# First k group of a hybrid decoder layer in seven products, their sums in three PSUM banks

## The chip, the cores and the metric

One core of one Trainium2 chip runs the whole layer. The metric is device time in microseconds, the median of several runs. The engines are named as the profile names them: PE is TensorE, DVE VectorE, ACT ScalarE, POOL GpSimd, SP SyncE.

## What is computed

The sizes: 512 tokens, model width 2048, 16 heads of 64, all in float32. The reference, cut:

```python
h = rms_norm(x, norm_g)
z = h @ w_in                       # 2048 -> 7 x 1024
a_val, a_glu, a_gate, q, k, v, b_gate = jnp.split(z, SPLIT_POINTS, axis=-1)
u = a_val * jax.nn.sigmoid(a_glu)
u = causal_depthwise_conv(u, conv_w, conv_b)              # 31 taps
u = jax.nn.silu(layer_norm(u, conv_norm_g, conv_norm_b))
u = u @ conv_pw_w + conv_pw_b
y_a = u * jax.nn.silu(a_gate)
q = rms_norm(q.reshape(bsz, s, N_HEADS, HEAD_DIM), q_norm_g)
k = rms_norm(k.reshape(bsz, s, N_HEADS, HEAD_DIM), k_norm_g)
o = dilated_attention_mixture(q, k, v)                    # windows (128,1) (512,4) (2048,16)
y_b = o.reshape(bsz, s, ATTN_WIDTH) * jax.nn.silu(b_gate)
y = x + jnp.concatenate([y_a, y_b], axis=-1) @ w_out
```

## The kernel before

**Matrix products.** Each float32 operand is split into a high and a low float16 part, and a product is three matmuls: high × high, high × low, low × high (`tri`, L409). The columns of the weights are worked off in groups of 512, in the order of GROUPS (L48): vg0 to vg3 (GLU value and gate), q0, k0, v0, bg0 (gate of attention), q1, k1, v1, ag0, ag1 (gate of the convolution branch), bg1, pw0, pw1 (pointwise), then the groups of the output product. vg0 and vg1 are done otherwise, in exact float32 parts.

An ordinary group has 4 units of 8 slots, one unit for 512 rows of weights (a tile wf, 1 MB). A slot is 6 matmuls of 512 columns (`slot_matmuls`, L884), so a group has 192. The weights of the next unit are split during a unit: ScalarE writes the high part wh (`split_hi`, L299), VectorE the low part wl (`split_lo`, L307), 2048 elements a partition each.

A group of SEVEN (L53: vg3, q0, v0) multiplies in halves of blocks: the weights give four blocks a11, a12, a21, a22, the activations b11 to b22, and seven products of sums of them stand for eight of blocks (`input_products`, L1106 to 1270). Each product has two pairs of 512 rows and two halves m, so 28 steps of 12 matmuls of 256 columns, 336. s1 to s4 are sums of weight blocks, t1 to t4 of activation blocks (`sum_x`, computed once, kept in tx). The sums s2, s3, s4 are made by accumulating DMAs that POOL issues (L1122), s1 by VectorE. For each product and pair ScalarE writes the high part (L1128) and VectorE, a step later, the low part of the weights, both named ws and 1024 wide; high parts are issued 5 steps ahead of the matmuls that read them. They come from a pool of four buffers. The products lie in banks of PSUM (lin_ps, four banks, tile ps_l), and are joined to the four output blocks cb by VectorE (`stt`, one operand in PSUM) and by copies of ScalarE (L1180).

**Norms of q and k.** `norm_qk` (L470 to 497): VectorE sums squares by head (`reduce`, tile ss), POOL scales and takes the power −1/2 (L478, L168), VectorE scales (cb or z times ss), ScalarE and VectorE write high and low parts qhl, SP transposes them. The four steps are due at the four delays of n, in slots.

**What sets the order.** One program is written out in one order; each engine takes its own instructions in that order. `clock[0]` counts slots; `after(n, fn)` puts work into a calendar for n slots later. A seven-product group counts 28 steps on 32 slots. Attention over half of the heads (`attention`, L792) is entered in the calendar when its k group has been issued, and starts at least 28 slots later.

The depthwise convolution is a generator (`conv`, from L537): 240 steps cv<-u,cw,cv on VectorE, then sums, LayerNorm (mean, squares lnsq, second moments, lnrow), the silu (L601) and the split into u16 (L314 high, then low). `run_conv` (L847) draws steps in each slot. A counter V.load adds an estimate of nanoseconds for every VectorE instruction, and each call takes PACE (1230; PACE_2, 1480, once attention has begun) off it; steps are drawn while it is below zero. So the convolution fills what the groups leave of VectorE. A seven-product group calls it 28 times and an ordinary one 32 times. Ahead of each unit of pw0, `while need not in u16: next(convolution)` issues whatever is still missing of the first four u16, in one go.

In bg0, bg1, ag0 and ag1 ScalarE takes the silu of each output tile (gate, L465); in bg1 VectorE then multiplies it by the attention output and ScalarE sums its squares (junk<-gate, L190), which it does for the weights too (junk<-wf, called wsum in the order).

Of the kernel before, what the change touches and what calls it, by code (L numbers as in the profile page):

```python
# [12 lines left out]
F16 = mybir.dt.float16  # L13
# [6 lines left out]
P = 128  # L20
S = 512
D = 2048
C = 1024
# [29 lines left out]
SEVEN = (("vg", 3), ("q", 0), ("v", 0))  # L53
LAST_SEVEN = SEVEN[-1]
BY_DMA = ("s2", "s3", "s4")
# [29 lines left out]
def layer(ctx: ExitStack, tc: tile.TileContext, xt, w1, w2, w3, g_in, conv_w, conv_b,  # L85
# [273 lines left out]
    xn, tx = {}, {}  # L359

    def sum_x(j):
# [5 lines left out]
        to = tx[j] = (wide if j < 4 else att).tile([P, 4, 2, H], F16, name="tx", tag="wide" if j < 4 else "att")  # L367
        V.tensor_sub(t1, b11, b12)
        V.tensor_sub(t3, b12, b22)
        V.tensor_add(t2, b22, t1)  # L370
        V.tensor_sub(t4, b21, t2)
        both = lambda t: t.rearrange("p (n t) -> p n t", n=2)

        def high():
            for n, t in ((0, t12), (2, t34)):
                A.activation(to[:, n:n + 2, 0], both(t), AF.Copy)

        def low():
            for n, t in ((0, t12), (2, t34)):
                V.tensor_tensor(to[:, n:n + 2, 1], both(t), to[:, n:n + 2, 0], op=OP.subtract)  # L380
# [28 lines left out]
    def tri(ps, a, b, first, last):  # L409
        (ah, al), (bh, bl) = a, b  # L410
        T.matmul(ps, ah, bh, start=first, stop=False)  # L411
        T.matmul(ps, ah, bl, start=False, stop=False)  # L412
        T.matmul(ps, al, bh, start=False, stop=last)  # L413
# [87 lines left out]
    def evac_qk(half_i, t, ps, is_k):  # L501
# [10 lines left out]
        if is_k and ("v", half_i) in SEVEN:  # L512
            n = [4 + 5 * (t > 0), 10 + 2 * t + 2 * (t > 0), 11 + 2 * t + 2 * (t > 0), 13 + 2 * t + 2 * (t > 0)]
# [591 lines left out]

    def input_products(i0):  # L1106
# [5 lines left out]
        def block(name, pair):  # L1112
            b = PLACE.get(name, name)
            return raw[i0 + 2 * pair + (b[2] == "2")][:, :, H * (b[1] == "2"):][:, :, :H]

        def add(name, pair):
            if name == "s1":
                V.tensor_tensor(block("a11", pair), block("a22", pair), block("a11", pair), op=OP.subtract)
            else:
                x, to = SUMS[name]  # L1120
                if name in BY_DMA:
                    nc.gpsimd.dma_start(block(to, pair), block(x, pair), accum_op=OP.add)  # L1122
                else:
                    V.tensor_tensor(block(to, pair), block(to, pair), block(x, pair), op=OP.add)
# [5 lines left out]
        def lo(name, pair):  # L1130
# [3 lines left out]
            for j in range(4):  # L1134
                mine = ("s2", "s4") if j % 2 else ("s1", "s3")
# [6 lines left out]
        def x_part(name, pair, k):  # L1142

            if name[0] == "t":
                t = tx[4 * pair + k][:, int(name[1]) - 1]
                return t[:, 0], t[:, 1]
# [3 lines left out]
        order = [("p1", "a11", "b11"), ("u", "a22", "t4"), ("x", "a12", "b21"), ("p7", "s3", "t3"), ("p5", "s1", "t1"),  # L1150
                 ("p6", "s2", "t2"), ("z", "s4", "b22")]
        u_first = group != SEVEN[0]
        if u_first:
            order[:2] = order[1::-1]

        def product(n, pair, m):
            to, w, x = order[n]
            if (pair, m) == (0, 0):
                bank[to] = lin_ps.tile([P, 2, H], F32, name="ps_l", tag="ps_l")
            ps, ms = bank[to][:, m], slice(m * P, (m + 1) * P)  # L1160
            for k in range(KU):
                t, xs = weights[w, pair], x_part(x, pair, k)
                first, last_ = pair == m == k == 0, pair == m == 1 and k == KU - 1
                if by_token:
                    tri(ps, [x[:, ms] for x in xs], (t[:, 0, k], t[:, 1, k]), first, last_)
                else:
                    tri(ps, [t[:, j, k, ms] for j in range(2)], xs, first, last_)
# [10 lines left out]
        def copy(name):  # L1178
            t = got[name] = slot("cb")
            A.activation(t, bank.pop(name).rearrange("p m t -> p (m t)"), AF.Copy, scale=e["p"])  # L1180

        def stt(out, name, by, other, op):
            V.scalar_tensor_tensor(out, bank[name].rearrange("p m t -> p (m t)"), e[by], other, op0=OP.mult, op1=op)

        def first_block():
            got["11"] = slot("cb")
            stt(got["11"], "x", "p", got["p1"], OP.add)
            bank.pop("x")

# [12 lines left out]

        def sixth():
            t = got["21"] = got.pop("u")
            V.tensor_tensor(t, t, got.pop("p7"), op=OP.add)

        def final():
            stt(got["12"], "z", "p", got["12"], OP.add)
            bank.pop("z")
# [3 lines left out]
        def out(name):  # L1213
# [26 lines left out]
            else:  # L1240
# [10 lines left out]
                norm_qk(group, t, sq, [(2, 4, 5, 6), (2, 5, 6, 8), (3, 8, 9, 11), (2, 9, 10, 12)][n], to)  # L1251

        plan = [(2, scales_of), (4, lambda: copy(order[0][0])), (8, lambda: copy(order[1][0])), (12, first_block), (16, lambda: copy("p7")),
# [201 lines left out]
```

## Time and profile before

| | |
|---|---|
| three runs, median (range) | 817.75 us (817.4 to 818.01) |
| profiled execution, span | 815.8 us |
| median less this span | 1.95 us |
| granted TensorE clock, mean | 0.999 |
| instructions | 13495 |

The time of the profiled execution is known by its span alone, from its first to its last instruction; what lies around the span is taken from the median. In the rows of the profile L12 is line 12 of the kernel; a row of the timeline has the start, the duration, the engine, the line, the operation with out<-in and, in brackets, the idle time ahead of it and what ended it. Durations of neighbours overlap a little on ScalarE and VectorE, so that the distance of two starts is the price of one.

### The profile page before, as it was taken

The page shows a single profiled execution, that of the slowest core. Times are in us where ns is not written, and L with a number is a line of the kernel's source. Part 1 is how long each engine was busy: PE and PEld are TensorE (multiplying, and loading weights), DVE is VectorE, ACT ScalarE, POOL GpSimd, SP SyncE. Part 2 cuts the span into 40 slices and gives each one's busy share as a digit, 9 for nine tenths or more (in the row PEclk, how much of TensorE's full clock was granted, in tenths as well). Part 3 has the DMA queues.
Part 4 walks back from the last instruction along what each step waited for, and adds up shares of the span by engine and source line. Part 5 has one row for each costly group of instructions (what it writes and reads, how often), then busy time and mean ns, then how long its engine had stood idle before and what let it go on. Part 6 is the DMA issues. An engine that isn't in the chain of part 4 may idle for free.

```text
span 815.8 us, 13495 instructions
## 1 busy us (share of the span) xinstructions
PE 807.9 (99%) x5271; PEld 500.6 (61%) x5271; DVE 707.1 (87%) x1181; ACT 553.6 (68%) x778; POOL 138.1 (17%) x159
## 2 busy tenths in 40 slices
PE   9999999999999999999999999999999999999998
PEld 6887645888646864444444444444444444788887
DVE  6768999889888989999999988996677798998985
ACT  6667687567656678677756748487688858766540
POOL 0001020413223500004112010010110002412420
PEclk9999999999999999999999999999999999999999
DMA  9953343995675862537473632536343477578752
GB/s 341 344 215 102 105 110 98 132 279 113 261 143 114 156 252 98 122 104 174 136 181 100 172 105 86 134 104 168 104 117 104 136 236 234 116 176 189 130 104 66
DMA packets 98625, 125.62 MB, mean 154 GB/s; under 512 B 62720, under 2 KB 83968, under 8 KB 89344
## 3 DMA queue, kind: packets, MB, share of 16 engines
q1 hardware_dynamic: 80800, 107.38, 41.9%
q0 software_dynamic: 17472, 17.30, 14.9%
q8 instruction: 41, 0.67, 0.3%
q14 instruction: 24, 0.20, 0.1%
q10 hardware_dynamic: 288, 0.07, 0.0%
HBM read 88.56 MB, written 4.19 MB: 114 GB/s over the span
## 4 chain that ended last, share of the span: by engine, by line
PE 69%; DVE 19%; ACT 5%; issue 3%; DMA 3%; POOL 1%; SPq 0%; ACTq 0%; DVEq 0%; POOLq 0%
PE ps_l L411 17%; PE ps_l L412 17%; PE ps_l L413 16%; PE ps_l L879 10%; DVE cv L80 6%; DVE wl L80 3%; DVE ws L80 3%; ACT junk L190 2%; PE ps_s L413 2%; PE ps_s L411 2%; PE ps_s L412 2%; PE ps_s L723 2%; PE ps_o L763 2%; DMA wf<-w_dram 1%; DVE cb L80 1%
## 5 line engine op out<-in xcount | busy, mean ns | idle before, releaser
L80 DVE SCALAR_TENSOR_TENSOR cv<-u,cw,cv 128x511 f32<-128x511 f32 (+14 forms) x240 | 162.2, 728 | 0.4 <-ACT cv L544 0.4
L190 ACT ACTIVATE junk<-wf 128x2048 uint8<-128x2048 f32 x68 | 129.2, 1900 | 3.5 <-DMA wf<-w_dram 3.1
L411 PE MATMUL ps_l<-x,wh 128*128 128x512 f16 x320 | 121.4, 379 | 0.3 <-DVE glu L80 0.3
L413 PE MATMUL ps_l<-x,wl 128*128 128x512 f16 x320 | 121.3, 379 | 0.0
L412 PE MATMUL ps_l<-x,wh 128*128 128x512 f16 x320 | 121.3, 379 | 0.0
L299 ACT ACTIVATE wh<-wf,ws 128x2048 f16<-128x2048 f32 x44 | 87.7, 1993 | 49.0 <-PE ps_l L412 49.0
L80 DVE SCALAR_TENSOR_TENSOR wl<-wf,ws,wh 128x2048 f16<-128x2048 f32 x45 | 105.6, 2347 | 13.0 <-ACT wh L299 13.0
L411 PE MATMUL ps_l<-wh,x 128*128 128x512 f16 x256 | 97.1, 379 | 0.0
L412 PE MATMUL ps_l<-wl,x 128*128 128x512 f16 x256 | 97.1, 379 | 0.0
L413 PE MATMUL ps_l<-wh,x 128*128 128x512 f16 x256 | 97.0, 379 | 0.0
L80 DVE SCALAR_TENSOR_TENSOR ws<-wf,ws 128x1024 f16<-128x1024 f32 x70 | 89.0, 1278 | 7.5 <-ACT ws L1128 4.9
L411 PEld LDWEIGHTS <-wh 128*128 128x128 f16 x480 | 47.0, 98 | 55.4 <-issue 3.5
L413 PEld LDWEIGHTS <-wl 128*128 128x128 f16 x480 | 46.9, 98 | 53.6 <-DVE wl L80 0.4
L412 PEld LDWEIGHTS <-wh 128*128 128x128 f16 x480 | 46.9, 98 | 50.4 <-issue 0.7
L879 PE MATMUL ps_l<-xr,wr 128*128 128x512 f32 x288 | 69.7, 397 | 0.1
L204 POOL TENSOR_SCALAR ws<-ws 128x1 f32<-128x1 f32 x22 | 10.7, 485 | 341.8 <-DVE ws L80 313.0
L879 PEld LDWEIGHTS ps_l<-xr,wr 128*128 128x128 f32 x288 | 54.1, 189 | 13.8 <-ACT xr L338 1.0
L413 PEld LDWEIGHTS <-x 128*128 128x128 f16 x352 | 34.4, 98 | 32.8 <-issue 1.5
L411 PEld LDWEIGHTS <-x 128*128 128x128 f16 x352 | 34.4, 98 | 32.4 <-issue 1.9
L412 PEld LDWEIGHTS <-x 128*128 128x128 f16 x352 | 34.4, 98 | 30.6 <-issue 0.5
L946 ACT ACTIVATE ws<-wf,ws 128x1024 f16<-128x1024 f32 x28 | 32.1, 1147 | 28.7 <-PE ps_l L413 9.4
L1128 ACT ACTIVATE ws<-wf,ws 128x1024 f16<-128x1024 f32 x42 | 46.4, 1138 | 6.1 <-PE ps_l L413 3.9
(250 smaller groups left out, 1823.3 us busy)
## 6 DMA issues: line engine op xcount, KB each, us to landing
wf<-w_dram SPq DMA_DIRECT2D x72, 1024.0 KB, 5.2
wf<-wf POOLq DMA_DIRECT2D x30, 512.0 KB, 6.5
x<-xt_dram SPq DMA_DIRECT2D x16, 256.0 KB, 6.7
res<-xt_dram SPq DMA_DIRECT2D x8, 512.0 KB, 6.5
out_dram<-res SPq DMA_DIRECT2D x15, 256.0 KB, 2.2
wf<-w_dram SPq DMA_DIRECT2D x7, 512.0 KB, 7.2
wf<-wf POOLq DMA_DIRECT2D x6, 256.0 KB, 6.3
qk<-qhl SPq DMA_TRANSPOSE x40, 3.0
```

The source lines that it names most:

```text
L80: return getattr(self.engine, name)(out, src, *args, **kw)
L190: A.activation(junk[:, :n], src, AF.Square, scale=scale, accum_out=acc)
L204: G.tensor_scalar(scale, scale, 1e-30, 2.0 ** (-2 * top), op0=OP.max, op1=OP.mult)
L299: A.activation(parts[i][0], raw[i], AF.Copy, scale=wscale[units[i][3:]][0])
L411: T.matmul(ps, ah, bh, start=first, stop=False)
L412: T.matmul(ps, ah, bl, start=False, stop=False)
L413: T.matmul(ps, al, bh, start=False, stop=last)
L723: T.matmul(ps[i, a], qk["q", hf][q][rows, p4, i * P:w], qk["k", hf][k][rows, p4, :w], start=n == 0, stop=n == 2)
L763: T.matmul(po[rows, i * P:(i + 1) * P], vs[hf][j // 2][:, j % 2, 2 * p4 + a, vp * DH:(vp + 1) * DH], got["t", a][:, pp * (ALL // P) + FROM ...
L879: T.matmul(banks[group, m], wt[:, a, m * P:(m + 1) * P], xk[b], start=k == 0 and a == b == 0, stop=k == KC - 1 and a == 1)
L946: A.activation(t[:, 0], block(name), AF.Copy, scale=wscale["wa", g][0])
L1128: A.activation(t[:, 0], block(name, pair), AF.Copy, scale=wscale[group][0])
```

## The change

k0 joins SEVEN, so that four seven-product groups stand in a row: vg3, q0, k0, v0. In all four the products are taken in a new order (ORDER) and accumulate in three banks: A gets a11·b11, then s2·t2, then s3·t3 and a22·t4, and is copied out between; B gets s1·t1, then s4·b22; C gets a12·b21. The signs of t2, t3 and t4 are turned for that. tx lies in pairs of tiles of two pools. s1, s2, s4 are made by DMA, s3 by VectorE. VectorE's joining instructions in a group go from five with an operand in PSUM and two without to two and one; ScalarE's copies from three to five. The four norms of a group by tokens all have the delays (2, 4, 5, 6). The delays that `evac_qk` had for k0 as an ordinary group are gone. The high and low part of s2 are issued one step later than the rule.

```diff
-SEVEN = (("vg", 3), ("q", 0), ("v", 0))
+SEVEN = (("vg", 3), ("q", 0), ("k", 0), ("v", 0))
-BY_DMA = ("s2", "s3", "s4")
...
         V.tensor_sub(t1, b11, b12)
-        V.tensor_sub(t3, b12, b22)
-        V.tensor_add(t2, b22, t1)
-        V.tensor_sub(t4, b21, t2)
+        V.tensor_sub(t3, b22, b12)
+        V.scalar_tensor_tensor(t2, t1, -1.0, b22, op0=OP.mult, op1=OP.subtract)
+        V.scalar_tensor_tensor(t4, t2, -1.0, b21, op0=OP.mult, op1=OP.subtract)
...
         n = [2, 6 + 4 * t, 7 + 4 * t, 9 + 4 * t]
-        if is_k and ("v", half_i) in SEVEN:
-            n = [4 + 5 * (t > 0), 10 + 2 * t + 2 * (t > 0), 11 + 2 * t + 2 * (t > 0), 13 + 2 * t + 2 * (t > 0)]
...
+    IN_SUMS = {"s1": ("a22", "a21"), "s2": ("a21", "a11"), "s4": ("a11", "a12")}
+    IN_PLACE = {"s1": "a21", "s2": "a11", "s3": "a21", "s4": "a12"}
+    ORDER = (("A", "a11", "b11"), ("B", "s1", "t1"), ("A", "s2", "t2"), ("C", "a12", "b21"), ("A", "s3", "t3"),
+             ("B", "s4", "b22"), ("A", "a22", "t4"))
...
-            if name == "s1":
-                V.tensor_tensor(block("a11", pair), block("a22", pair), block("a11", pair), op=OP.subtract)
+            if name == "s3":
+                V.tensor_tensor(block("a21", pair), block("a11", pair), block("a22", pair), op=OP.subtract)
...
-            if (pair, m) == (0, 0):
+            to, w, x = ORDER[n]
+            if to not in bank:
                 bank[to] = lin_ps.tile([P, 2, H], F32, name="ps_l", tag="ps_l")
...
+        def copy(to, name, by="p"):
+            got[to] = slot("cb")
+            A.activation(got[to], flat(name), AF.Copy, scale=e[by])
+
+        def joint(to, name, other):
+            got[to] = got.pop(other)
+            V.scalar_tensor_tensor(got[to], flat(name), e["p"], got[to], op0=OP.mult, op1=OP.add)
+            bank.pop(name)
+
+        def fourth():
+            p5 = got.pop("p5")
+            got["22"] = got.pop("nw")
+            V.tensor_tensor(got["22"], got["22"], p5, op=OP.subtract)
+
+        def third():
+            copy("21", "A", "n")
+            bank.pop("A")
...
-                norm_qk(group, t, sq, [(2, 4, 5, 6), (2, 5, 6, 8), (3, 8, 9, 11), (2, 9, 10, 12)][n], to)
-
-        plan = [(2, scales_of), (4, lambda: copy(order[0][0])), (8, lambda: copy(order[1][0])), (12, first_block), (16, lambda: copy("p7")),
-                (25, joint), (26, fifth), (27, sixth), (29, final), (30, lambda: out("12"))]
-        plan += [(26 if kind == "v" else 13, lambda: out("11")), (27, lambda: out("22")), (28, lambda: out("21"))]
+                norm_qk(group, t, sq, (2, 4, 5, 6), to)
+
+        plan = [(2, scales_of), (4, lambda: copy("p1", "A")), (8, lambda: copy("p5", "B")), (12, lambda: copy("u2", "A")),
+                (16, lambda: joint("11", "C", "p1")), (17, lambda: out("11")),
+                (20, lambda: copy("nw", "A", "n")), (21, fourth), (22, lambda: out("22")),
+                (24, lambda: joint("12", "B", "u2")), (25, lambda: out("12")), (28, third), (29, lambda: out("21"))]
...
-        sums = ((-2, "s2", 0), (-1, "s2", 1), (5, "s4", 0), (7, "s4", 1), (6, "s1", 0), (8, "s1", 1)) if u_first else (
-            (3, "s2", 0), (4, "s2", 1), (8, "s4", 0), (9, "s4", 1), (9, "s1", 0), (11, "s1", 1))
         plan += [(n, lambda name=name, pair=pair: add(name, pair))
-                 for n, name, pair in ((-8, "s3", 0), (-7, "s3", 1)) + sums]
+                 for n, name, pair in ((-8, "s1", 0), (-7, "s1", 1), (-3, "s2", 0), (-1, "s2", 1),
+                                       (6, "s3", 0), (8, "s3", 1), (9, "s4", 0), (11, "s4", 1))]
```

What moves on the engines, at two places. The first is ScalarE at the end of bg1 and ahead of pw0. L601 (L600 in the changed kernel) is the silu of a LayerNorm tile cv, L314 (L313) the high part u16 made from it; a gate is one output tile of bg1, in the order of the tokens. Before, from the first u16 to the second gate:

```order
L314 ACTIVATE u16_6012<-cv_1215,us_671 128x512
L601 ACTIVATE cv_2963<-cv_2963,lnb_98,lng_97 128x512
L314 ACTIVATE u16_6033<-cv_1217,us_671 128x512
L299 ACTIVATE wh_6044<-wf_5161,ws_5471 128x2048
L601 ACTIVATE cv_2965<-cv_2965,lnb_98,lng_97 128x512
L314 ACTIVATE u16_6060<-cv_2963,us_671 128x512
L465 ACTIVATE gate_6068<-ps_l_5671,esc_6069 128x512
L190 ACTIVATE junk_125,ysumab_6076<-gate_6068 128x512
L601 ACTIVATE cv_3745<-cv_3745,lnb_98,lng_97 128x512
L190 ACTIVATE junk_125,wsum_6089<-wf_5975 128x2048
L314 ACTIVATE u16_6093<-cv_2965,us_671 128x512
L465 ACTIVATE gate_6101<-ps_l_5769,esc_6069 128x512
```

Now, from the row behind the first gate and its sum of squares on:

```order
L407 ACTIVATE lnrow_6169<-ps_s_6237 128x512
L189 ACTIVATE junk_125,wsum_6247<-wf_6128 128x2048
L466 ACTIVATE gate_6257<-ps_l_5918,esc_6226 128x512
L189 ACTIVATE junk_125,ysumab_6232<-gate_6257 128x512
L466 ACTIVATE gate_6274<-ps_l_5938,esc_6226 128x512
L600 ACTIVATE cv_1215<-cv_1215,lnb_98,lng_97 128x512
L466 ACTIVATE gate_6292<-ps_l_5982,esc_6226 128x512
L600 ACTIVATE cv_1217<-cv_1217,lnb_98,lng_97 128x512
L313 ACTIVATE u16_6296<-cv_1215,us_671 128x512
L600 ACTIVATE cv_3441<-cv_3441,lnb_98,lng_97 128x512
L313 ACTIVATE u16_6300<-cv_1217,us_671 128x512
L600 ACTIVATE cv_3443<-cv_3443,lnb_98,lng_97 128x512
```

The four u16 that pw0's first unit reads stood ahead of the second gate; now lnrow, which all silus need, stands between the first and the second gate, and the u16 behind the fourth. The third and the fourth u16 follow below, each behind a silu.

The second place is VectorE at a norm. ss is the sum of squares, cb a block of q or k, ws a low part of weights. The first norm of q0 before:

```order
L80 TENSOR_REDUCE ss_1995<-sq_1993 128x8
L80 SCALAR_TENSOR_TENSOR ws_1996<-wf_1107,ws_1340,ws_1996 128x1024
L80 SCALAR_TENSOR_TENSOR cv_1217<-u_570,cw_95,cv_1217 128x501
L80 TENSOR_TENSOR cb_1975<-cb_1975,ss_1995 128x512
L80 SCALAR_TENSOR_TENSOR ws_2026<-wf_1014,ws_1340,ws_2026 128x1024
```

The third and fourth norm of k0 now (qg is the weight of the norm):

```order
L79 TENSOR_REDUCE ss_2690<-sq_2687 128x8
L79 TENSOR_TENSOR qhl_2720<-cb_2589,qhl_2720 128x512
L79 TENSOR_TENSOR cb_2465<-cb_2465,ss_2690 128x512
L79 SCALAR_TENSOR_TENSOR ws_2726<-wf_1975,ws_2397,ws_2726 128x1024
L79 TENSOR_TENSOR cb_2747<-cb_2747,qg_100 128x512
L79 TENSOR_TENSOR qhl_2762<-cb_2465,qhl_2762 128x512
L79 SCALAR_TENSOR_TENSOR ws_2764<-wf_2102,ws_2397,ws_2764 128x1024
L79 TENSOR_REDUCE ss_2769<-sq_2766 128x8
L79 TENSOR_TENSOR cb_2747<-cb_2747,ss_2769 128x512
```

Between a reduction and the scaling that needs POOL's answer to it stood a low part and a convolution step; now there is one small instruction, and in the last norm none.

82 lines of the change are left out of this document (26 added, 56 removed).

## Prediction

> **What bounds the kernel now.** I read the page first, then the waits of TensorE, then the stages by windows. The page's busy times:
>
> ```profile
> span 815.8 us, 13495 instructions
> PE 807.9 (99%) x5271; PEld 500.6 (61%) x5271; DVE 707.1 (87%) x1181; ACT 553.6 (68%) x778; POOL 138.1 (17%) x159
> ```
>
> TensorE is the bound. VectorE, at 87%, is its only near rival. The three runs of before have a median of 817.75 us, 1.95 more than this span. I make the sum against the span and add 1.95. About 0.2%, 1.64 us, is what can be told from no change.
>
> Two things can move the end: matmul time, and time in which TensorE waits. What it waits for from 95 to 700 us (us in total, times, longest):
>
> ```profile
> PE ps_l L412 <- DVE ws L80: 1.8, 2, 1.1
> PE ps_s L568 <- DVE lnacc L80: 0.8, 1, 0.8
> PE ps_l L411 <- ACT ws L1128: 0.4, 1, 0.4
> PE ps_l L411 <- DVE glu L80: 0.3, 1, 0.3
> ```
>
> So a microsecond on another engine is free unless it ends in such a wait, and any new wait is paid in full. The windows of q0 (seven products), k0 (eight) and v0 (seven), one row each: length, then busy time and count of PE, PEld, DVE, ACT, POOL:
>
> ```profile
> 175.31:212.02 36.71, 36.71 (x340) 32.86 (x338) 32.14 (x40) 24.94 (x28) 9.69 (x9) 1.00 0.68 151
> 212.02:253.48 41.46, 41.46 (x195) 18.78 (x193) 36.89 (x52) 24.51 (x25) 9.80 (x12) 1.00 0.67 182
> 253.48:293.24 39.76, 37.51 (x339) 32.84 (x337) 34.25 (x42) 25.18 (x30) 18.35 (x15) 1.00 0.82 188
> ```
>
> q0 runs without a wait. v0 does the same number of matmuls and takes 39.76 − 36.71 = 3.05 us longer: the weight waits (the two ws rows above) and shorter pauses.
>
> **Part 1: k0 in seven products.** It removes 192 matmuls of 512 columns and adds 336 of 256: k0 becomes a q0. Gain 41.46 − 36.71 = 4.75 us. That holds if the weights are in time, which is part 3.
>
> **Part 2: where the convolution goes.** VectorE fills each step up to a budget of estimated time with convolution steps. The rows of VectorE's forms (138 to 294 us, but the first, which is the page's):
>
> ```profile
> L80 DVE SCALAR_TENSOR_TENSOR cv<-u,cw,cv 128x511 f32<-128x511 f32 (+14 forms) x240 | 162.2, 728 | 0.4 <-ACT cv L544 0.4
> L80 DVE SCALAR_TENSOR_TENSOR ws<-wf,ws 128x1024 f16<-128x1024 f32 x41 | 52.1, 1278 | 4.9 <-ACT ws L1128 4.9
> L80 DVE SCALAR_TENSOR_TENSOR cb<-ps_l,esc,cb 128x512 f32<-128x512 f32 x8 | 5.9, 743 | 0.0
> L80 DVE TENSOR_TENSOR cb<-cb 128x512 f32<-128x512 f32 x5 | 3.4, 688 | 0.1
> L80 DVE TENSOR_TENSOR cb<-cb,ss 128x512 f32<-128x512 f32 x4 | 2.7, 687 | 1.5 <-POOL ss L168 1.5
> ```
>
> A seven-product group needs 14 low parts of 1278 ns, 17.9 us, where k0 has four of 2349 ns in before; so little is left for the convolution. By the order of both programs k0 holds 26 of its 240 steps before and 5 after, and at the end of v0 the convolution is 21 or 22 steps behind: 21 × 0.68 us (162.2 / 240) = 14.2 us of VectorE work. Later groups make it up slowly, as their budget was used already. The last step moves from slot 16 of ag1 to slot 30, the second moments of LayerNorm from slot 10 of bg1 to 22. What is then left is forced out at once ahead of pw0's first matmul (the `while need not in u16` loop). The rows of ScalarE's order that stand with the change show it at the end of bg1. Three of the four high parts u16 that pw0 needs stood ahead of bg1's first gate, the fourth just behind it; now all four gates stand ahead of the first u16, as ScalarE takes its rows in order. The rows of before around pw0's start give the prices (ScalarE, VectorE, TensorE):
>
> ```profile
> 607.50 0.69 ACT L465 ACTIVATE gate<-ps_l,esc 128x512 f32<-128x512 f32 x1 [1.71 <-POOL esc L424]
> 609.01 0.63 ACT L190 ACTIVATE junk<-gate 128x512 uint8<-128x512 f32 x1 [0.82 <-DVE gate L80]
> 609.63 0.80 ACT L601 ACTIVATE cv<-cv,lnb,lng 128x512 f32<-128x512 f32 x1
> 610.34 1.90 ACT L190 ACTIVATE junk<-wf 128x2048 uint8<-128x2048 f32 x1
> 612.23 0.71 ACT L314 ACTIVATE u<-cv,us 128x512 f16<-128x512 f32 x1
> 612.84 0.67 ACT L465 ACTIVATE gate<-ps_l,esc 128x512 f32<-128x512 f32 x1
> 612.97 0.75 DVE L80 SCALAR_TENSOR_TENSOR u<-cv,us,u 128x512 f16<-128x512 f32 x1 [0.87 <-ACT u L314]
> 611.98 0.38 PE L411 MATMUL ps_l<-u,wh 128*128 128x512 f16 x1
> 614.16 0.38 PE L412 MATMUL ps_l<-u,wh 128*128 128x512 f16 x1
> 616.36 0.67 ACT L465 ACTIVATE gate<-ps_l,esc 128x512 f32<-128x512 f32 x1
> 616.93 0.80 ACT L601 ACTIVATE cv<-cv,lnb,lng 128x512 f32<-128x512 f32 x1
> 617.64 0.71 ACT L314 ACTIVATE u<-cv,us 128x512 f16<-128x512 f32 x1
> 618.25 0.67 ACT L465 ACTIVATE gate<-ps_l,esc 128x512 f32<-128x512 f32 x1
> ```
>
> From start to start a gate takes 0.57, its sum of squares 0.62, a silu 0.71, a u16 0.61, the weights' sum 1.89. Call T0 the start of pw0's first matmul if nothing waited (611.98 here). The fourth tile's second operand is wanted at 614.16, T0 + 2.18. In before its low part ended at 612.97 + 0.75 = 613.72, only 0.44 us ahead.
>
> After, counted from the start of the first gate: 0.57 + 0.62; lnrow 0.57 (priced as a gate, the same shape read from PSUM); sum 1.89; gate and its squares 1.19, gate 0.57, silu 0.71, gate 0.57, silu 0.71; then u16, silu, u16, silu, u16, silu, u16 = 4 × 0.61 + 3 × 0.71 = 4.57. Together 11.97; two waits of 0.82 to 0.91 for VectorE's product ahead of the squares, 1.7; the low part 0.75; hand-over 0.2. That is 14.6 us. The first gate starts at T0 − 4.48 as in before (607.50, after its wait for POOL), or at the earliest at about T0 − 6.3 (token 0 is done 36 matmuls of 0.2155 before T0, and the order puts a table load ahead of it). So the fourth low part ends at T0 + 8.3 to 10.1, and TensorE waits 6.1 to 7.9 us. The floor is set by the fourth gate alone, which follows bg1's last matmul: from T0 + 0.3, 0.57 + 0.71 + 4.57 + 0.95 = T0 + 7.1, a wait of 4.9. I take **6.5**, near the end that the whole queue gives; range 4.9 to 7.9. No wait behind it can take it back, since the view of TensorE's waits has no row at all from 612 us to the end.
>
> **Part 3: the four groups and their norms.** The new sums leave a group two products from PSUM and one difference where there were five and two: 3 × 743 + 688 = 2.9 us less of VectorE in each; two more copies on ScalarE are hidden (it is busy 24.94 of 36.71). The sums' DMAs are as many in a group, six; k0's six are new on POOL's queue. Against it stands the spacing of the norms. One in q0 (VectorE, POOL):
>
> ```profile
> 195.00 0.68 DVE L80 TENSOR_REDUCE ss<-sq 128x8 f32<-128x512 f32 x1
> 195.77 1.21 POOL L478 TENSOR_SCALAR ss<-ss 128x8 f32<-128x8 f32 x1 [3.00 <-DVE ss L80]
> 197.06 2.02 POOL L168 TENSOR_TENSOR ss<-ss,half 128x8 f32<-128x8 f32 x1
> 199.11 0.69 DVE L80 TENSOR_TENSOR cb<-cb,ss 128x512 f32<-128x512 f32 x1 [1.54 <-POOL ss L168]
> ```
>
> The chain through POOL takes 199.11 − 195.68 = 3.4 us; VectorE had 1.9 us of work behind the reduction and stood still for 1.54. The rows of VectorE's order that stand with the change have this norm before and two of k0 after.
>
> POOL's two instructions for a norm, over the eight of 138 to 294 us:
>
> ```profile
> L478 POOL TENSOR_SCALAR ss<-ss 128x8 f32<-128x8 f32 x8 | 5.0, 628 | 40.6 <-DVE ss L80 40.6
> L168 POOL TENSOR_TENSOR ss<-ss,half 128x8 f32<-128x8 f32 x8 | 14.8, 1853 | 0.7
> ```
>
> Their means make a chain of 0.63 + 1.85 = 2.5 us. Of k0's norms the third has 0.69 us of VectorE's work between, the fourth nothing; the other six of q0 and k0 have by the order 2.0, 2.0, 0.7, 1.5 and 2.0, 2.7. So VectorE would wait 0.5 + 0.5 + 1.8 + 1.0 in q0 and 0.5 + 0 + 1.8 + 2.5 in k0, 8.6 us, where the row of before shows 1.5: 7.1 more, on an engine behind which the low parts queue. The new sums free 2 × 2.9 = 5.8 in the same two groups. The rest, 1.3, is lateness if all of it reaches TensorE; q0 hid its 1.5 in before, so I take about half. The stalls of k0 and v0 then are 3.8 against 3.05: **+0.75**. Ends: −3.05 (all gone), and +4.8 if four of the eight chains take 3.4 us as the one shown (0.8 + 4 × 1.0). Attention(0) starts 8 slots earlier; k's last transposes are issued at slot 7 of v0, 16 slots ahead of it: nothing.
>
> **Sum.** −4.75 + 6.5 + 0.75 = +2.5: span 818.3, time **820.3 us**.
>
> **The rivals.** (a) *Seven products starve in a row* (slower): the norms' waits come back as lateness in k0 and v0, +4.8 in place of +0.75: −4.75 + 6.5 + 4.8 = +6.55, 824.3 us. With pw0's wait at its floor of 4.9 it alone makes the kernel slower by over 1.64 once the added stalls pass 1.5 us, which is 0.1 us more on each of the eight chains than the 2.5 (0.75 + 8 × 0.1). For it: v0 is late in before. Against: q0 is not. 0.12.
> (b) *The clock cools in pw0's wait* (slower): the first rows of the trace show matmuls at half pace after idleness:
>
> ```profile
> 0.98 4.02 PE L146 MATMUL ps_s<-wz 128*128 128x512 f16 x9 [0.98 <-POOL wz L143]
> 5.07 5.16 PE L879 MATMUL ps_l<-xr,wr 128*128 128x512 f32 x20
> ```
>
> Nine matmuls in about 4 us, 0.45 each against 0.2155: half of 4.02, 2.0 us, is lost. If a 6.5 us wait does that again the time is 822.3. No wait of before exceeds 1.1 us here, so the trace can't tell from which length on. 0.12. The Trainium skill, “TensorE: Matmul & The Clock Gate”, Part 1, puts the array back to half rate after an idle window of about 3.4 us, until it was busy as long; by that rule rival (b) would be certain with a wait of twice the window and the sum 822.3; the trace agrees with the slow start's length and shows nothing of the return.
> (c) *It cancels* (no change): the wait at its floor, 4.9, stalls as now: +0.15, 817.9. 0.22.
> (d) *Faster*: VectorE's freed time ends v0's 3.05 us of stalls and the wait is at its floor: −4.75 − 3.05 + 4.9 = −2.9, 814.9. It needs a wait under 6.2 with the stalls gone; if ScalarE got through LayerNorm in time at all, 813.0 with stalls as now. 0.18.
> That k0 isn't in seven products is excluded by the order: 336 matmuls of 256 columns stand in it.
>
> **How the numbers follow.** The forecast has 0.36. Slower: 0.36 + 0.12 + 0.12 = 0.60; same, (c), 0.22; faster, (d), 0.18. The range reaches from 815.5, between (d) and (c), to just above (a)'s 824.3. The slower cases alone span 819.4 to 824.5.
>
> **What would show it.** Right: k0's window at 36.7 to 37.5 us; a TensorE wait of about 6.5 us for u at pw0's start, with lnrow and four silus packed just before; VectorE idle behind POOL's ss at the third and fourth norms. Wrong: no wait for u there (then the queue's count failed), or stalls in k0 and v0 above 5 us, or 512-column matmuls at 0.43 us after the wait.

## The result and the profile after

The changed kernel takes 846.43 us (four runs, 845.46 to 847.65) against 817.58 for the kernel before: ratio 1.0353, 95% interval 1.0338 to 1.0367. It is 28.9 us slower; 820.3 was forecast, with 824.5 as the upper end. The profiled execution took 846.12 us and has a span of 844.3, 28.5 more than the 815.8 of before. I account for these 28.5.

The page of the kernel after:

```profile
span 844.3 us, 13837 instructions
PE 814.7 (96%) x5415; PEld 517.9 (61%) x5415; DVE 713.0 (84%) x1184; ACT 567.5 (67%) x799; POOL 145.7 (17%) x166
```

ScalarE has 14 us more work than before (567.5 after 553.6), VectorE 6 (713.0 after 707.1). TensorE is busy for 7 us more in a span 28.5 longer: it waits. Its waits from 95 to 700 us, the six largest (us in total, times, longest):

```profile
PE ps_l L413 <- DVE ws L79: 12.1, 9, 4.1
PE ps_l L412 <- ACT u L313: 3.1, 1, 3.1
PE ps_l L414 <- DVE wl L79: 2.5, 2, 1.8
PE ps_l L412 <- ACT ws L1129: 2.0, 2, 1.7
PE ps_s L722 <- DVE gate L79: 1.5, 1, 1.5
PE ps_s L393 <- DVE lnacc L79: 1.4, 1, 1.4
```

The forecast wait for u at pw0 is there (3.1), but the low parts ws of the groups cost four times as much. By stages, the windows of q0, k0, v0, bg0, of q1 to ag1 together, of bg1 and pw0 (each from a group's first matmul to that of the next; a row has the length, busy time and count of PE, PEld, DVE, ACT and POOL, the granted clock, the DMA engines' busy share and GB/s):

```profile
175.87:215.25 39.38, 37.34 (x339) 32.87 (x337) 30.70 (x39) 25.73 (x30) 13.31 (x13) 1.00 0.79 167
215.25:266.13 50.88, 41.52 (x339) 34.92 (x337) 37.48 (x46) 32.90 (x39) 22.52 (x20) 0.90 0.89 180
266.13:308.51 42.38, 39.59 (x363) 33.61 (x361) 31.18 (x40) 27.86 (x32) 10.26 (x11) 1.00 0.93 191
308.51:359.56 51.05, 46.27 (x279) 21.12 (x277) 45.77 (x91) 37.87 (x53) 0.97 (x3) 1.00 0.40 112
359.56:584.05 224.49, 223.62 (x1304) 103.66 (x1303) 217.13 (x384) 153.89 (x231) 29.56 (x36) 1.00 0.51 136
584.05:638.27 54.22, 49.75 (x294) 23.21 (x292) 36.55 (x81) 39.40 (x62) 7.16 (x10) 0.97 0.38 104
638.27:665.41 27.14, 26.53 (x181) 12.06 (x181) 22.04 (x46) 23.36 (x39) 0.95 (x3) 0.94 0.21 70
```

The same from bg0 on in the kernel before (q0, k0 and v0 are in the prediction):

```profile
293.24:336.76 43.52, 43.52 (x220) 19.50 (x217) 42.35 (x77) 36.28 (x50) 1.86 (x3) 1.00 0.52 145
336.76:565.30 228.54, 227.75 (x1390) 106.35 (x1389) 219.25 (x399) 159.08 (x241) 30.07 (x36) 1.00 0.49 132
565.30:611.98 46.68, 46.68 (x291) 22.48 (x290) 28.95 (x68) 35.45 (x52) 6.92 (x10) 1.00 0.35 96
611.98:636.58 24.60, 24.60 (x183) 11.84 (x182) 20.39 (x45) 22.48 (x39) 0.94 (x3) 1.00 0.33 110
```

So: q0, k0, v0 take 132.6 us where 117.9 stood, +14.7; bg0 +7.5; q1 to ag1 −4.05; bg1 and pw0 54.22 + 27.14 − 46.68 − 24.60 = +10.1. Together 28.25 of the 28.5. I call what the three groups take over 36.71 each (q0's window without a wait) their stalls: 132.64 − 110.13 = 22.5 us, against 3.05 in the one that stalled before. Then 14.7 is −4.75, the gain of k0, and +19.5 of stalls.

How a stall comes about is seen at the largest one, TensorE's wait of 4.06 us at 261.35. The rows of VectorE, ScalarE, POOL and TensorE in time:

```profile
250.49 0.68 DVE L79 TENSOR_REDUCE ss<-sq 128x8 f32<-128x512 f32 x1
251.96 2.58 POOL L167 TENSOR_TENSOR ss<-ss,half 128x8 f32<-128x8 f32 x1
254.57 0.69 DVE L79 TENSOR_TENSOR cb<-cb,ss 128x512 f32<-128x512 f32 x1 [1.56 <-POOL ss L167]
255.29 0.63 ACT L487 ACTIVATE qhl<-cb 128x512 f16<-128x512 f32 x1 [4.42 <-DVE cb L79]
256.87 1.89 ACT L189 ACTIVATE junk<-wf 128x2048 uint8<-128x2048 f32 x1
258.76 0.61 ACT L1226 ACTIVATE sq<-cb 128x512 f32<-128x512 f32 x1
259.41 0.69 DVE L79 TENSOR_TENSOR cb<-cb,qg 128x512 f32<-128x512 f32 x1 [2.76 <-ACT sq L1226]
260.02 1.28 DVE L79 SCALAR_TENSOR_TENSOR ws<-wf,ws 128x1024 f16<-128x1024 f32 x1
261.35 0.37 PE L413 MATMUL ps_l<-ws,tx 128*128 128x256 f16 x1 [4.06 <-DVE ws L79]
```

VectorE waits for POOL; ScalarE, which takes its queue in order, waits 4.42 us for VectorE with a high part, a sum of weights and the next square queued behind; VectorE then waits 2.76 us for that square; and the low part that TensorE wants stands behind all of it. VectorE, the busiest of the three, stands idle for over 4 of these 11 us (1.56 + 2.76 in the brackets). At this place it is a chain handed from queue to queue, not a lack of time.

### The profile page after: what moved, and what is told of

Same layout as the page of the kernel before. It is cut to its first block, busy times and chain, and to the rows that moved or that the text cites. A ratio compares the mean times of both kernels' runs of the same rounds, so it can differ in the third digit from the quotient of the medians.

```text
span 844.3 us, 13837 instructions
## 1 busy us (share of the span) xinstructions
PE 814.7 (96%) x5415; PEld 517.9 (61%) x5415; DVE 713.0 (84%) x1184; ACT 567.5 (67%) x799; POOL 145.7 (17%) x166
## 4 chain that ended last, share of the span: by engine, by line
PE 57%; DVE 15%; ACT 12%; DMA 8%; issue 4%; POOL 2%; SPq 1%; ACTq 0%; POOLq 0%; DVEq 0%
PE ps_l L412 13%; PE ps_l L413 13%; PE ps_l L414 13%; PE ps_l L878 10%; DMA wf<-wf 5%; DVE cv L79 4%; DVE wl L79 3%; ACT junk L189 3%; ACT wh L298 2%; ACT sx L734 2%; PE ps_s L413 2%; PE ps_s L412 2%; DVE ws L79 2%; PE ps_s L414 2%; PE ps_s L722 1%
## 5 line engine op out<-in xcount | busy, mean ns | idle before, releaser
L79 DVE SCALAR_TENSOR_TENSOR ws<-wf,ws 128x1024 f16<-128x1024 f32 x84 | 107.0, 1278 | 13.1 <-ACT ws L1129 10.5
L79 DVE SCALAR_TENSOR_TENSOR wl<-wf,ws,wh 128x2048 f16<-128x2048 f32 x41 | 96.3, 2348 | 12.9 <-ACT wh L298 12.7
L298 ACT ACTIVATE wh<-wf,ws 128x2048 f16<-128x2048 f32 x40 | 79.8, 1995 | 39.6 <-PE ps_l L413 39.5
L1129 ACT ACTIVATE ws<-wf,ws 128x1024 f16<-128x1024 f32 x56 | 62.4, 1139 | 23.6 <-DMA wf<-wf 16.9
L413 PE MATMUL ps_l<-wl,x 128*128 128x512 f16 x192 | 72.8, 379 | 0.2 <-DVE wl L79 0.2
L412 PE MATMUL ps_l<-wh,x 128*128 128x512 f16 x192 | 72.8, 379 | 0.0
L414 PE MATMUL ps_l<-wh,x 128*128 128x512 f16 x192 | 72.8, 379 | 0.0
L413 PE MATMUL ps_l<-ws,tx 128*128 128x256 f16 x192 | 54.2, 282 | 11.3 <-DVE ws L79 11.2
L412 PE MATMUL ps_l<-ws,tx 128*128 128x256 f16 x192 | 54.1, 282 | 2.0 <-ACT ws L1129 2.0
L414 PE MATMUL ps_l<-ws,tx 128*128 128x256 f16 x192 | 54.2, 282 | 0.0
L945 ACT ACTIVATE ws<-wf,ws 128x1024 f16<-128x1024 f32 x28 | 32.1, 1147 | 28.1 <-PE ps_l L414 9.5
```

The lines of the kernel that those rows point to most:

```text
L79: return getattr(self.engine, name)(out, src, *args, **kw)
L298: A.activation(parts[i][0], raw[i], AF.Copy, scale=wscale[units[i][3:]][0])
L412: T.matmul(ps, ah, bh, start=first, stop=False, skip_group_check=more)
L413: T.matmul(ps, ah, bl, start=False, stop=False, skip_group_check=more)
L414: T.matmul(ps, al, bh, start=False, stop=last, skip_group_check=more)
L945: A.activation(t[:, 0], block(name), AF.Copy, scale=wscale["wa", g][0])
```

## The experiments

Each is one run beside the kernel before, which took 817.1 to 817.8 us in these. The changed kernel's own four runs lie 2.2 us apart, so I read nothing from less. The table has the time and the sums of windows as above (stalls of q0, k0, v0; with k0 an ordinary group, its 41.47 us stand for one 36.71).

| kernel | us | stalls | bg0 | q1 to ag1 | bg1 + pw0 |
|---|---|---|---|---|---|
| before | 817.6 | 3.0 | 43.5 | 228.5 | 71.3 |
| after | 846.4 | 22.5 | 51.1 | 224.5 | 81.4 |
| three_new | 823.7 | 9.7 | 43.5 | 227.6 | 71.3 |
| four_old | 847.1 | 16.5 | 52.0 | 226.0 | 86.1 |
| spread | 844.6 | 22.0 | 51.1 | 224.5 | 80.4 |
| copies | 844.3 | 21.9 | 51.1 | 224.5 | 80.4 |
| no_sums | 839.2 | 14.4 | 51.0 | 224.5 | 82.0 |
| no_pool | 837.8 | 14.8 | 51.0 | 224.5 | 81.4 |
| s4_dve | 843.7 | 19.4 | 51.1 | 224.6 | 82.0 |
| pace1540 | 844.3 | 21.8 | 51.4 | 233.0 | 71.3 |
| no_sums_pool | 832.9 | 7.1 | 52.7 | 224.6 | 81.7 |
| none3 | 832.4 | 4.7 | 51.1 | 226.2 | 82.7 |
| qg_late | 846.1 | 22.5 | 51.1 | 224.5 | 81.7 |
| att_late | 839.4 | 21.3 | 43.8 | 229.8 | 78.4 |
| combo1 | 833.3 | 18.4 | 43.5 | 233.9 | 71.3 |
| combo4 | 838.5 | 22.2 | 43.5 | 233.9 | 71.3 |
| three_s4 | 822.2 | 8.1 | 43.5 | 227.6 | 71.3 |
| three_s24 | 823.5 | 9.9 | 43.5 | 227.6 | 71.3 |
| clean | 818.0 | 2.5 | 43.5 | 234.6 | 71.3 |

**Which half of the change: three_new, four_old.** My theory after the result was that two groups by tokens side by side, q0 and k0, are the cause; the rival was the new order and banks. three_new:

```diff
-SEVEN = (("vg", 3), ("q", 0), ("k", 0), ("v", 0))
+SEVEN = (("vg", 3), ("q", 0), ("v", 0))
```

> The changed kernel with k0 an ordinary group again: the new order, banks and signs in vg3, q0 and v0 alone. Theory A (two groups by tokens in seven products side by side are the cause: their norms, transposes and sums fill queues that one such group leaves free): k0 lasts 41.5 us again, the stalls of q0 and v0 together stay under 5 us, time 815 to 820 us. Theory B (the new order and banks themselves are the cause): q0 and v0 keep the 2.7 and 5.7 us of stalls they have in the changed kernel, or more, and the time is over 824 us.

four_old, from the kernel before:

```diff
-SEVEN = (("vg", 3), ("q", 0), ("v", 0))
+SEVEN = (("vg", 3), ("q", 0), ("k", 0), ("v", 0))
-                norm_qk(group, t, sq, [(2, 4, 5, 6), (2, 5, 6, 8), (3, 8, 9, 11), (2, 9, 10, 12)][n], to)
+                norm_qk(group, t, sq, (2, 4, 5, 6), to)
```

> The kernel before with k0 in seven products and nothing else new but the delays (2, 4, 5, 6) for all norms of such groups: the old order, seven banks' worth of products, old signs and sums. Theory A (two such groups side by side): k0 lasts 47 us or more and the time is 835 us or more, as with the new banks. Theory B (the new order and banks): k0 lasts under 39 us and the time is under 822 us, the rest being pw0's wait.

four_old takes 847.1 us: with the old order k0 in seven products costs as much. By its stages it isn't what I expected (k0 43.49, v0 46.40, and 86.1 in bg1 and pw0, as its convolution ends only in bg1); by the total, theory A holds. three_new takes 823.7, between the two: the new order alone costs 6.5 us, in q0 (40.16), k0 (43.63) and v0 (40.76). So k0 in seven products costs 22.7 us with the new order (846.4 − 823.7) and 29.5 with the old, where the norms' delays changed too; the new order costs 6.5 while k0 is an ordinary group, and nothing once it isn't.

**Where in q0 and k0: spread, copies.** spread gives the norms the delays they had before:

```diff
-                norm_qk(group, t, sq, (2, 4, 5, 6), to)
+                norm_qk(group, t, sq, [(2, 4, 5, 6), (2, 5, 6, 8), (3, 8, 9, 11), (2, 9, 10, 12)][n], to)
```

> The changed kernel with the four norms of a group spread as before: (2,4,5,6), (2,5,6,8), (3,8,9,11), (2,9,10,12). Theory A1 (VectorE and ScalarE stand still behind POOL's answer because reduction and scaling are too near): VectorE's wait for ss falls from 10.7 us to under 4 and the time by 5 to 12 us. Theory A2 (the transposes of q and k hold the temporary buffers, or the accumulating DMAs of the sums are late): the time stays within 3 us of 846, or rises, since the buffers are held longer.

VectorE's waits (175 to 310 us) and the largest of ScalarE, in spread:

```profile
DVE cb L79 <- POOL ss L167: 3.7, 3, 1.6
ACT ws L1129 <- DMA wf<-wf: 23.0, 11, 4.8
```

and in the changed kernel (175 to 309):

```profile
DVE cb L79 <- POOL ss L167: 10.7, 7, 2.1
DVE cb L79 <- ACT sq L1226: 3.9, 2, 2.8
ACT ws L1129 <- DMA wf<-wf: 16.5, 7, 4.6
```

The wait for POOL fell as theory A1 said, and the time by 1.8 us only (844.6, where A1 had 5 to 12 less): ScalarE now waits 6.5 us more for the sums' DMAs. Here a wait that went turned up as the next. copies replaces the transposes:

```diff
-                        nc.sync.dma_start(store[:, 2 * x:2 * x + 2, f:f + P], src[:, m * H:(m + 1) * H], transpose=True)
+                        nc.sync.dma_start(store[:, 2 * x:2 * x + 2, f:f + P], src[:, m * H:(m + 1) * H].rearrange("p (a b) -> p a b", a=2))
```

> The changed kernel with the transposes of q0 and k0 by SP replaced by plain copies of the same bytes to the same places, so q and k reach attention untransposed. Theory A2a (transposes: they are slow to issue and land, and hold ScalarE's temporary buffers): the stalls of q0, k0, v0 fall from 22.5 us to under 10 and the time to 833 us or less. Theory A2b (the accumulating DMAs of the sums come late through POOL's queue and busy DMA engines): the stalls stay above 18 us, the time above 841.

844.3 us, stalls 21.9: that q and k are transposed has no part in it that one run can show.

**The sums and POOL: no_sums, no_pool, no_sums_pool, s4_dve.** no_sums leaves the accumulating DMAs out:

```diff
             else:
-                x, to = IN_SUMS[name]
-                nc.gpsimd.dma_start(block(to, pair), block(x, pair), accum_op=OP.add)
+                pass
```

> The changed kernel without the accumulating DMAs of s1, s2 and s4 in its four groups (the products then take the blocks as they lie, so the result is another). Theory A2b (the sums come late: POOL issues them behind norms, they land late, ScalarE's high parts wait for them, and everything behind): the stalls of q0, k0, v0 fall from 22.5 us to under 5, and bg0's too; 820 to 827 us, what is left being pw0's wait. Theory A3 (VectorE has no time for four such groups in a row, whatever the DMAs do): stalls stay above 12 us, time above 833.

no_pool leaves POOL's part of the norms out:

```diff
-            G.tensor_scalar(ss, ss, f / DH, f * RMS_EPS, op0=OP.mult, op1=OP.add)
-            rsqrt(ss)
+            if store not in SEVEN:
+                G.tensor_scalar(ss, ss, f / DH, f * RMS_EPS, op0=OP.mult, op1=OP.add)
+                rsqrt(ss)
...
-            V.tensor_mul(by_head(z), by_head(z), ss[:, :, None].to_broadcast([P, 8, DH]))
+            by = ones[:, :8] if store in SEVEN else ss
+            V.tensor_mul(by_head(z), by_head(z), by[:, :, None].to_broadcast([P, 8, DH]))
```

> The changed kernel without POOL's two instructions in the norms of q0 and k0; VectorE scales by ones in their place, all else stays. Theory A1 (waits of VectorE for POOL's answer make the low parts late): stalls fall from 22.5 us to under 10, time to 833 or less. Theory A2b (the sums): POOL is free of the norms but the sums land as late as their own transfers take, so that the stalls fall by 2 to 8 us only, time 836 to 843.

no_sums_pool has both edits.

> The changed kernel without the accumulating DMAs of its four groups and without POOL's part in the norms of q0 and k0 (both left out as in the runs that left out one; the result is another). Each alone took 8 us of the 22.5 us of stalls in q0, k0, v0. Theory A4 (two separate lateness sources on one in-order chain): together they take 14 to 18, leaving 5 to 9 us; time 829 to 833 us. Theory A5 (both are one path, POOL's queue): together hardly more than one, 12 to 14 us left, time 836 to 839.

TensorE's waits for low parts from 175 to 310 us, in no_sums, no_pool and no_sums_pool:

```profile
PE ps_l L413 <- DVE ws L79: 9.0, 8, 1.7
```

```profile
PE ps_l L413 <- DVE ws L79: 8.7, 8, 2.4
```

```profile
PE ps_l L413 <- DVE ws L79: 3.4, 5, 1.1
```

Alone each takes 8 us from the stalls (22.5 to 14.4 and 14.8), together 15.4 (to 7.1). Theory A4 holds: two sources on one in-order chain, which add up. That the sums alone were the cause (no_sums under 5) and that POOL alone was (no_pool under 10) both fell; for no_pool the time was where A2b had it. By itself no_sums came out in the ranges of theory A3 (VectorE has no time); but no_sums_pool leaves VectorE's instructions as they are and has 7.1 us of stalls left, so its time isn't the main cause. Why spread, which takes 7.0 us off VectorE's waits for POOL, gains so much less than no_pool stays open: no run has spread's delays without the sums. s4_dve makes one sum on another engine:

```diff
+                if name == "s4":
+                    nc.vector.tensor_tensor(block(to, pair), block(to, pair), block(x, pair), op=OP.add)
+                else:
-                nc.gpsimd.dma_start(block(to, pair), block(x, pair), accum_op=OP.add)
+                    nc.gpsimd.dma_start(block(to, pair), block(x, pair), accum_op=OP.add)
```

> The changed kernel with s4 made by VectorE (two additions of 1.2 us a group) where POOL issued a DMA. s4 is issued at steps 9 and 11 and read at 15 and 17, the nearest of the three sums. Theory A2b: ScalarE no longer waits for it, stalls fall by 5 us or more, time under 841. Theory A3 (VectorE's time): stalls grow by about the 2.4 us a group that VectorE gets, time 846 to 853.

843.7 us, stalls 19.4: the direction of A2b and 3 of the 5 us, so neither theory's range was met. ScalarE's waits for the sums' DMAs (16.5 us in the changed kernel) are gone, but its waits for VectorE's cb (rows sq and v) grew from 6.8 to 21.2: the lateness was handed on again.

**The weight of k's norm: none3, qg_late.** none3 is no_sums_pool without these lines:

```diff
-                if kind == "k":
-                    V.tensor_mul(by_head(t), by_head(t), gp[:, None, :].to_broadcast([P, 8, DH]))
```

> As the run without sums and without POOL's part, and also without k0's multiplication by the norm's weight on VectorE (four of 0.69 us, each behind ScalarE's square of the same block; the result is another). Theory A6 (this multiplication makes VectorE wait for ScalarE, which k0 as an ordinary group didn't): stalls fall by 4 us or more against that run. Theory A3 (VectorE has simply too little time): they fall by no more than the 2.8 us of the four multiplications.

qg_late is the changed kernel with

```diff
-                    V.tensor_mul(by_head(t), by_head(t), gp[:, None, :].to_broadcast([P, 8, DH]))
+                    after(1, lambda: V.tensor_mul(by_head(t), by_head(t), gp[:, None, :].to_broadcast([P, 8, DH])))
```

> The changed kernel with k0's multiplication by the norm's weight issued one slot later, so that ScalarE has read the block by then. Theory A6: VectorE's wait for ScalarE's square (3.9 us before) goes and the stalls of k0 and v0 fall by 3 to 6 us, time 840 to 843. Against it: the low parts are late for the sums' and POOL's sake and take no notice, 845 to 847.

none3's stalls are 4.7 us, 2.4 below, which is no more than the multiplications' own time, and its time is only 0.5 below. qg_late takes 846.1: k0 is shorter (44.85), v0 longer (48.36), the sum the same. Its waits for ScalarE's square fell from 3.9 to 2.0 us (the longest from 2.8 to 1.1) and didn't go, as A6 had it. The stalls took no notice of the 1.9 us, so theory A6 falls as far as these two runs can tell.

**bg0: att_late.**

```diff
-        start = max(clock[0] + 28, max(at_pair.values(), default=0) + PERIOD[0])
+        start = max(clock[0] + 29, max(at_pair.values(), default=0) + PERIOD[0])
```

> The changed kernel with attention(0) begun 8 slots later, where it began in the kernel before (the bound of 28 slots made 29). bg0 lasted 51.05 us in every run of the changed kernel whatever the stalls ahead of it, and 43.5 with k0 an ordinary group. Theory C (the early start puts attention's VectorE work on top of v0's last norms and outputs, and the low parts of bg0 come late): bg0 falls to 43.5 to 45 us, the later groups rise by about 3, time 840 to 843. Theory D (bg0 is late because VectorE comes late out of v0): bg0 stays above 49 us.

839.4 us. The window of bg0 in it:

```profile
306.81:350.65 43.84, 43.69 (x219) 19.43 (x217) 41.95 (x76) 37.25 (x51) 1.79 (x3) 1.00 0.50 136
```

43.84 where it was 51.05, at stalls of 21.3 ahead of it: theory C. Counted from k0's first slot, the start was put at 58 instead of 66 by a rounding (`(PHASE - start) % 8`), as a seven-product group ends its count one slot earlier. In the changed kernel 4.7 us of bg0 are waits of TensorE (for wl 2.5, gate 1.5, wh 0.4, st 0.3), and it holds 279 matmul records where 220 stood: attention's, which later groups then lack.

**The end of bg1: pace1540.**

`run_conv` (it begins at L853; L847, named above, is in the lines ahead of it) gets more to draw:

```diff
-PACE_2 = 1480
+PACE_2 = 1540
```

> The changed kernel with PACE_2 at 1540 in place of 1480, which draws more of the convolution in each slot once attention has begun; LayerNorm and the u16 then stand at the end of bg1 as in the kernel before. If pw0's wait comes from the convolution that the four groups push back, the waits for lnacc (1.4 us) and u (3.1 + 0.6 us) and the half clock at 621 and 638 us (2.8 us) all go: 836 to 839 us. If the wait comes from lateness carried out of k0 and v0, it stays: above 843.

bg1 and pw0 fall to 71.3 us, as in before, to the tenth: their 10.1 us come from the convolution pushed back, as the first sentence expected, and not from lateness out of v0. The total falls by 2.2 us only, because q1 to ag1 grow by 8.5; by the time alone (844.3) the run would have spoken for the other theory.

**Repairs together: combo1, combo4; and without k0: three_s4, three_s24.** combo1 is att_late, s4_dve and PACE_2 1540; combo4 adds s2 on VectorE and delays (2, 5, 6, 7); the other two are three_new with s4, or s2 and s4, on VectorE as in s4_dve.

> The changed kernel with three of the repairs: attention(0) 8 slots later, s4 by VectorE, PACE_2 1540. Alone they gave 7.0, 2.7 and 2.2 us. If the terms are separate: bg0 at 43.5 to 44, bg1 and pw0 at 46.7 and 24.6 without a loss in q1 to ag1 (attention isn't early any more), so 7.0 + 2.7 + about 7 = 17 us less, 828 to 832 us, still slower than before, since the stalls of q0, k0, v0 stay near 19. If one lateness is handed on: under 10 us less, above 836.

> As combo1, and s2 by VectorE too, and the norms one slot further between reduction and scaling: (2, 5, 6, 7). If the sums' transfers and POOL's answers are the lateness, the stalls of q0, k0, v0 fall by 4 us or more against combo1, to under 15, time 823 to 827. If VectorE's time is now the limit (2.4 us a group more for the sums), they stay or grow: 828 to 834.

> The new order with k0 an ordinary group, s4 by VectorE. That kernel without this took 823.7 us, 6.5 more than before, in q0 (+3.45), k0 (+2.2) and v0 (+1.0). If the transfer of s4, issued six steps ahead of its use, is the cause, 818 to 821 us; if it isn't, 823 to 827.

> As three_s4 with s2 by VectorE as well. If the sums are the whole cause: 815 to 818.5 us, no worse than before. If the norms' common delays (2, 4, 5, 6) have a part of it: 819 to 822.

combo1 gets 13.1 us back, to 833.3: bg0 and bg1 with pw0 are as in before, but the pace costs 5.4 in q1 to ag1, which I had at none, and so it misses the range that I gave. combo4 is worse, 838.5 (stalls 22.2), above both of its ranges. VectorE's time is not the limit there: it is busy for 113.6 of the 132.4 us of q0, k0 and v0. From 175 to 310 us it has a wait that combo1 hasn't:

```profile
DVE wf L1126 <- DMA wf<-wf: 9.0, 3, 4.1
```

L1126 is a sum on VectorE, s2 at all three places. s2 adds to a11 the block in which s1 is made, and s1 still comes by DMA; whatever VectorE has to do next stands behind that wait. combo4 also has other delays than combo1, so that its loss isn't split between the two. three_s4 takes 822.2, between its two ranges, and three_s24 823.5, above both: the transfer of s4 explains 1.5 of the new order's 6.5 us at most, s2's nothing. What the rest of these 6.5 is stays open.

**Everything away: clean.** It has none3's omissions (sums, POOL's part, weight of k's norm), attention later and PACE_2 1520:

> The changed kernel with everything that was found taken away at once: no accumulating DMAs in the four groups, no POOL in the norms of q0 and k0, no weight multiplication in k0 (left out as before, so the result is another), attention(0) 8 slots later, PACE_2 1520. If these are all the causes: stalls of q0, k0, v0 at 4 to 6 us, bg0 43.5, bg1 and pw0 46.7 and 24.6, up to 5 us more than before in v1 to ag1 for the pace; 815 to 821 us. If something else has a part: above 823.

818.0 us, in the expected range. Its windows of k0, v0 and of q1 to ag1:

```profile
211.99:249.95 37.96, 37.02 (x339) 32.89 (x337) 33.60 (x42) 30.11 (x36) 1.76 (x2) 1.00 0.51 148
249.95:287.89 37.94, 37.03 (x340) 32.91 (x338) 33.95 (x43) 27.89 (x32) 2.14 (x4) 1.00 0.51 156
331.41:565.97 234.56, 230.77 (x1391) 106.88 (x1389) 227.53 (x413) 159.97 (x241) 31.23 (x36) 0.99 0.48 131
```

Stalls are 2.5 us and k0 has its gain: 5.3 us over the three groups (−4.75 and −0.55). VectorE is busy for 100.1 of their 112.6 us, as long as in the changed kernel (99.4 of 132.6): as much of its work fits. The gain is all lost in q1 to ag1, +6.0, where VectorE is busy for 227.5 of 234.6 us: the convolution that k0 no longer holds has to go somewhere, and the groups behind have no room. No run was faster than the kernel before.

## Why the prediction was wrong

Slower was forecast for pw0's sake, and that part held; the largest part of the loss came out of the step that I had priced at 0.75 us.

**Part 1, k0's gain of 4.75 us: right.** clean shows it, by what it leaves out. "That holds if the weights are in time" was the condition, and it failed.

**Part 2, the convolution pushed to pw0: right, and not the whole.** I forecast a wait of 6.5 us (4.9 to 7.9) for pw0's four tiles. The rows of ScalarE, VectorE and TensorE there:

```profile
628.32 0.69 ACT L466 ACTIVATE gate<-ps_l,esc 128x512 f32<-128x512 f32 x1
634.82 0.38 PE L414 MATMUL ps_l<-x,wl 128*128 128x512 f16 x1
636.23 0.67 ACT L466 ACTIVATE gate<-ps_l,esc 128x512 f32<-128x512 f32 x1
637.50 0.72 ACT L313 ACTIVATE u<-cv,us 128x512 f16<-128x512 f32 x1
638.27 0.58 PE L412 MATMUL ps_l<-u,wh 128*128 128x512 f16 x1 [3.07 <-ACT u L313]
642.20 0.75 DVE L79 SCALAR_TENSOR_TENSOR u<-cv,us,u 128x512 f16<-128x512 f32 x1 [0.56 <-ACT u L313]
```

bg1's last matmul starts at 634.82, so pw0's first could have started at T0 = 635.04. The first gate stands 6.7 us ahead of that, just beyond the early end that I gave, and the fourth low part is done at 642.20 + 0.75, T0 + 7.9, where I had 8.3 to 10.1. TensorE lost 3.23 us ahead of pw0's first matmul and 27.14 − 24.60 = 2.54 in pw0, 5.8 in all. What I missed is the rest of the 10.1 us that bg1 and pw0 lost: LayerNorm's sum is late in bg1 too (lnacc, 1.4 us), the clock halves behind it (1.6, below), and two matmuls of LayerNorm (ps_s<-lnacc,ones, 0.9) that stood ahead of bg1 before now stand in it. Some 0.4 is left.

**Part 3, the four groups: this step failed.** I wrote: "The new sums free 2 × 2.9 = 5.8 in the same two groups. The rest, 1.3, is lateness if all of it reaches TensorE; q0 hid its 1.5 in before, so I take about half." The term of +0.75 us measured +19.5. The waits of VectorE for POOL were near what I counted (10.7 us measured, 8.6 forecast). Setting them off against time freed was the error: VectorE stood idle a quarter of the time in the three groups, and freed time bought nothing (three_new frees as much in q0 and v0, and its stalls are 9.7 us where 3.0 stood), while a wait on a chain through three in-order queues is passed on (spread, s4_dve). POOL's part in the norms costs 7.7 us of stalls (no_pool). And "The sums' DMAs are as many in a group, six; k0's six are new on POOL's queue" was given no price; the sums of the four groups cost 8.1 us of stalls (no_sums). Each is read six to eight steps after its issue, and ScalarE, which waited for none of them in the kernel before, waits 16.5 us for them. k0's weight multiplication, which q0 hasn't, wasn't in the sum (2.4 us of stalls at most, none3). Rival (a), "seven products starve in a row", was the case; its price of 4.8 was a quarter of the 19.5 measured, because I bounded it by POOL alone.

**"Attention(0) starts 8 slots earlier ...: nothing": wrong.** I looked at the data it waits for and not at the VectorE work that it brings ahead. A start 8 slots later gives 7.0 us back (att_late), 5.0 of it in the stages behind (bg0 −7.2, q1 to ag1 +5.3, bg1 and pw0 −3.0); the rest is less than the runs of one kernel differ by.

**Rival (b), the clock: it came true, and not only at pw0.** TensorE's rows behind the long wait in k0, and a few later:

```profile
261.51 0.42 PE L414 MATMUL ps_l<-ws,tx 128*128 128x256 f16 x1
261.73 0.42 PE L412 MATMUL ps_l<-ws,tx 128*128 128x256 f16 x1
266.24 0.27 PE L413 MATMUL ps_l<-ws,x 128*128 128x256 f16 x1
266.35 0.27 PE L414 MATMUL ps_l<-ws,x 128*128 128x256 f16 x1
```

The starts are 0.215 apart, then 0.109 again. Over the four stretches at half pace, 50 matmuls are spaced at double: 37 of 256 columns × 0.104 and 13 of 512 × 0.211 is 6.6 us, part of the stalls and of what bg1 and pw0 lost above. The Trainium skill, “TensorE: Matmul & The Clock Gate”, Part 1, says the clock halves after an idle window of about 3.4 us; the trace agrees with the length of a half-paced stretch (3.4 us at 621) but shows one behind a wait of 1.4 us, so the measurement decides: a shorter wait was enough there.

## What to carry to other kernels

A stage whose engines hand work round in order (a low part behind a norm behind another engine's answer behind a DMA) can be bounded by its latencies while no engine is busy throughout: price a new step by the whole loop it joins, and don't set freed time of an engine that idles against it. When a filler such as the convolution loses its room, look where it goes: if the groups behind are full, it costs time there (6.0 us in clean) or at the end (10.1 in the changed kernel). A start that moves because a count rounds differently belongs in the sum.

## What the runs showed of the hardware

The granted clock halved after less idleness than I expected. bg1's wait for LayerNorm's sum, by TensorE's rows:

```profile
617.20 0.38 PE L414 MATMUL ps_l<-x,wl 128*128 128x512 f16 x1
618.98 1.05 PE L393 MATMUL ps_s<-ones,lnacc 128*128 128x2 f32 x8 [1.41 <-DVE lnacc L79]
620.97 0.57 PE L414 MATMUL ps_l<-x,wl 128*128 128x512 f16 x1
621.76 0.63 PE L413 MATMUL ps_l<-x,wh 128*128 128x512 f16 x1
624.60 0.38 PE L414 MATMUL ps_l<-x,wl 128*128 128x512 f16 x1
```

A single wait of 1.41 us, 1.05 us of small matmuls and 1.1 of matmuls at full pace, and the next ones took 0.43 us each for 3.4 us. In the kernel before no wait exceeded 1.1 us, and the clock stayed whole from 5.6 to 814.5 us.

The length of one wait doesn't decide it. In three_new the matmuls behind one of 2.01 us are 0.21 us apart, and the clock stayed whole from 4.8 to 820.6 us:

```profile
218.32 0.38 PE L413 MATMUL ps_l<-wl,x 128*128 128x512 f16 x1 [2.01 <-DVE wl L79]
218.53 0.38 PE L414 MATMUL ps_l<-wh,x 128*128 128x512 f16 x1
```

The traces fit a grid. The half-paced stretches of the changed kernel begin at 231.91, 259.21, 621.03 and 638.09 us, that is 8, 106 and 5 times 3.413 us apart, and each lasts one or two times 3.41 us, as the window of the first:

```profile
231.91:235.32 3.41, 3.41 (x18) 2.41 (x17) 3.06 (x4) 3.41 (x6) 0.00 (x0) 0.50 0.21 42
```

So it seems to matter how a wait falls into such a step and how idle the step is; how much of a step must be idle was not measured here.
